# Two layers on one core: the order of seven weight products, and a tile of its own for a sum of weights

## The chip, the cores and the metric

The kernel runs on one core of one Trainium2 chip. TensorE (PE) multiplies matrices, VectorE (DVE) and ScalarE (ACT) do elementwise work, GpSimd (POOL) and SyncE (SP) mostly start transfers. The metric is the device time of one execution in microseconds (us). Beside the plain times there is one profiled execution, whose trace records what every engine did and when; all times within the program are counted from the start of its span.

## The reference

Two layers over 512 frames of width 1024, all in float32: the first with latent attention, the second with chunked attention, each followed by a SwiGLU feed-forward of inner width 2816. The feed-forward, which the change touches, is

```python
def rms_norm(x, g):
    xf = x.astype(jnp.float32)
    y = xf * lax.rsqrt(jnp.mean(xf * xf, axis=-1, keepdims=True) + EPS)
    return (y * g.astype(jnp.float32)).astype(x.dtype)
...
def swiglu(h, w_gate, w_up, w_down):
    return (jax.nn.silu(h @ w_gate) * (h @ w_up)) @ w_down
...
    for layer in range(DEPTH):
        h = rms_norm(x, attn_pre_g[layer])
        ...
        x = x + rms_norm(y, attn_post_g[layer])
        h = rms_norm(x, ffn_pre_g[layer])
        f = swiglu(h, ffn_w_gate[layer], ffn_w_up[layer], ffn_w_down[layer])
        x = x + rms_norm(f, ffn_post_g[layer])
```

## The kernel before

**Three matmuls for one.** A float32 operand is kept as a high part `hi` (rounded by a ScalarE cast, L144) and a low part `lo` (the rest, a VectorE subtraction, L145). Every product is hi·hi + lo·hi + hi·lo, three matmuls into the same bank of PSUM, the memory in which TensorE accumulates.

**Seven products for a pair of blocks.** The inner width 2816 is cut in 22 blocks of 128. The first four blocks are multiplied plainly (`proj`, L361 to L363; their gate is multiplied by the norm's factor at L1148, and L1151 forms the hidden block `hd`). The other 18 go in nine pairs of a gate and an up block through `products`. There the four quarter products of gate and up by the two halves of the frames (A0 and A1, 256 each) are had from seven products instead of eight, in Strassen's manner: sums of weights and sums of activations are multiplied, and the results are added up. Product j multiplies a weight tile `raw[j]` of 128x1024 by one of the lists in `moving`; it has two halves e of 12 matmuls each, which go to two banks. The banks are `be` for j0, `al` for j1, `ga` for j2, `al` for j3, j4 and j5, and `be` for j6. Several products thus accumulate in one pair of banks, and each is read out before the next is added to it: j0 and j1 by ScalarE copies (L1503, L1505), j2 by a VectorE addition to `gt` (L1507), j3 by a ScalarE copy to `gt` (L1509), j4 by a VectorE addition to `ut` (L1511), j5 by a ScalarE copy to `ut` (L1513), and j6 by a VectorE addition (L1515), which is followed by the norm's factor (L1516), silu (L1517), the product of gate and up (`hd`, L1519) and four sums of hidden blocks for the next stage (L1220 to L1223). `al` and `ga` come from a pool of four banks, which the plain blocks use as well, `be` from one of two other pairs of banks in turn.

**The weights.** Class `Pair` loads four tiles a pair (`tile`, L162, 512 KB each, started on SP's queue) and forms the others as sums on VectorE (L174): r0 = r4 + r5, r3 = r0 + r1, r6 = r3 + r2, and r4 becomes r4 + r1. r0, r3 and r6 share one tile ("sum", two buffers), since each is added in place to the one before. r4 lies in "sum2" (two buffers), r5, r1 and r2 in "raw" (five buffers). A load can start when a buffer is free, that is, when the last cast of its old contents is done.

**What sets the order.** `Feed` holds a plan: a list of all weight tiles in the order in which they are multiplied. `feed.next(1024, 2)` hands out the next one and, ahead of it, has the tile two places on split in hi and lo (with its sum) and the loads up to four places on started. The instructions of each engine are then put in an order by a scheduler with priorities, so that instructions of j6 may come ahead of those of j5, or those of one pair ahead of those of another. Each engine runs its list strictly in that order and waits where an operand is missing.

Behind `products` follows `down` (L1255), the last projection by a seven-product scheme of its own. In layer 1, `aside` runs beside `products`: it is advanced at the places where j is 1, 3 and 5, and brings the residual stream back in order of frames.

Of the kernel before, what the change touches and what calls it, by code (L numbers as in the profile page):

```python
# [10 lines left out]
F32 = mybir.dt.float32  # L11
# [7 lines left out]
D, S, P = 1024, 512, 128  # L19
# [49 lines left out]
def trunk(ctx: ExitStack, tc: tile.TileContext, a, out):  # L69
# [12 lines left out]
    def name_(n):  # L82
        uid[0] += 1
        return f"{n}_{uid[0]}"

    def U(dt=F32, name="u"):
        return up.tile([P, S], dt, tag="u", name=name_(name), bufs=NU)
# [4 lines left out]
    def bank(tag="mm", name="b"):  # L92
        return ps.tile([P, S], F32, tag=tag, name=name_(name), bufs={"mm": 4, "s": 2, "t": 2}[tag])
# [57 lines left out]
    class Pair:  # L151

        def __init__(self, src):
            self.src, self.raw = src, {}

# [13 lines left out]
        def sums(self, j):  # L172
            def plus(t, x, y):
                V.tensor_tensor(t, x, y, op=OP.add)  # L174

            r = self.raw
            if j == 0:
                r[0] = r[3] = r[6] = wide[0].tile([P, 1024], F32, tag="sum", name=name_("raw"), bufs=2)
                plus(r[0], r[4], r[5])
            elif j in (3, 6):  # L180
                plus(r[j], r[j], r[j // 3])
            elif j == 4:
                plus(r[4], r[4], r[1])

    wide = [None]

    class Down:
# [41 lines left out]
        def plus(self, j, i, x, y):  # L229

            x, t = self.at[x, i], self.at[y, i]
            n = max(len(x), len(t))
            cut_ = lambda v: v if len(v) == n else [v[0][:, c * S:c * S + S] for c in range(n)]
            for p, q in zip(cut_(t), cut_(x)):
                V.tensor_tensor(p, p, q, op=OP.add)
            self.at[j, i] = t
# [15 lines left out]
    class Feed:  # L252
# [8 lines left out]

        def add_pair(self, src):

            for j in range(7):
                self.plan.append((Pair(src) if not j else self.plan[-1][0], 1024, j, None))

        def add_down(self, src):
            d = Down(src)
# [73 lines left out]
        def next(self, n, ahead=True):  # L342
            i = self.pos
            self.pos += 1
            assert self.plan[i][1] == n
            self.split(i + int(ahead))
            return self.ready[i]
# [48 lines left out]
    def cut(t, c):  # L396
        return t[0][:, c], t[1][:, c]
# [97 lines left out]
    class Head:  # L495
# [3 lines left out]
        def __init__(self, qk, bt, scale, pv, sums):  # L499
            self.qk, self.bt, self.scale, self.pv, self.sums = qk, bt, scale, pv, sums  # L500
            self.p, self.pt = {}, None
# [538 lines left out]
    def start_a(h):  # L1040
# [12 lines left out]
        def pv(pth, ptl):  # L1053
            fill.until("v")
            o = bank()
            v_ = slice(h * VD, (h + 1) * VD)
            for kt in range(NQT):
                q_ = slice(kt * P, S)
                mm3(o[:, q_], (va[kt][:, 0, v_], va[kt][:, 1, v_]), (pth[:, kt, q_], ptl[:, kt, q_]),
                    kt == 0, kt == NQT - 1)  # L1060
            V.reciprocal(sums, sums)
            of = U(name="of")
            nc.scalar.copy(of, o)

            def rest():
                V.tensor_tensor(of, of, spread(sums), op=OP.mult)
                oh, ol = U(F32R, "oh"), U(F32R, "ol")
                split(oh, ol, of)
                osp.append((oh, ol))

            return rest
# [11 lines left out]
    def ffn(i, x_src, osp, firsts, late=()):  # L1083
# [55 lines left out]
        for f in range(N_WHOLE):  # L1139
# [13 lines left out]
            if f == 1:  # L1153
                next(more)
        products(xs, tb, rb, hid, by_tokens(H) if i else None)
        post = (AfterLast if i else After)(i, eps, H)
        down(hid, post)
# [311 lines left out]
    def products(xs, tb, rb, hid, aside=None):  # L1469

        K2 = KT // 2
        moving = [[cut(tb[k][0], A0) for k in range(K2)], [cut(xs[k], A0) for k in range(K2)],
                  [cut(xs[k + K2], A0) for k in range(K2)], [cut(tb[k][0], A1) for k in range(K2)],
                  [cut(tb[k][1], A0) for k in range(K2)], [cut(tb[k][1], A1) for k in range(K2)],
                  [cut(xs[k + K2], A1) for k in range(K2)]]
        pairs = (NF - N_WHOLE) // 2
        for p in range(pairs):
            al, ga = [], []
            be = [bank("t" if p % 2 else "s", "be") for _ in range(2)]
            gate = [U(name="gt") for _ in range(2)]  # L1480
            up_ = [U(name="ut") for _ in range(2)]
            for j in range(7):
                if aside is not None and j in (1, 3, 5):
                    next(aside, None)
                w = feed.next(1024, 2)
                if p + 1 == pairs and j >= 4:
                    hid.ahead(j // 5)
                if j == 1:
                    al = [bank(name="al") for _ in range(2)]
                if j == 2:  # L1490
                    ga = [bank(name="ga") for _ in range(2)]
                to = (be, al, ga, al, al, al, be)[j]
                for e in range(2):
                    o = to[e][:, A0]
                    for k in range(K2):
                        l, r = w(e * S + k * P, P), moving[j][k]
                        first_ = j < 3 and k == 0
                        for n, (c, d) in enumerate(((0, 0), (0, 1), (1, 0))):
                            nc.tensor.matmul(o, l[c], r[d], start=first_ and n == 0, stop=k == K2 - 1 and n == 2,  # L1499
                                             skip_group_check=True)  # L1500
                    t, u = gate[e], up_[e]
                    if j == 0:
                        nc.scalar.copy(u[:, A1], o)  # L1503
                    elif j == 1:
                        nc.scalar.copy(t[:, A0], o)  # L1505
                    elif j == 2:
                        V.tensor_tensor(t[:, A0], t[:, A0], o, op=OP.add)  # L1507
                    elif j == 3:
                        nc.scalar.copy(t[:, A1], o)  # L1509
                    elif j == 4:  # L1510
                        V.tensor_tensor(u[:, A1], o, u[:, A1], op=OP.add)  # L1511
                    elif j == 5:
                        nc.scalar.copy(u[:, A0], o)  # L1513
                    else:
                        V.tensor_tensor(t[:, A1], t[:, A1], o, op=OP.add)  # L1515
                        V.tensor_tensor(t, t, rb, op=OP.mult)  # L1516
                        nc.scalar.activation(t, t, AF.Silu)  # L1517
                        h = hid.room()
                        V.tensor_tensor(h, t, u, op=OP.mult)  # L1519
                        hid.add(h)  # L1520
# [274 lines left out]
```

## Time and profile before

| | us |
|---|---|
| median of 3 runs | 1112.13 (1111.6 to 1112.59) |
| the profiled execution | 1113.16 |
| its span | 1111.4 |
| `products` of layer 0 in it | 236.24 to 416.92 |
| `products` of layer 1 in it | 817.43 to 997.90 |

The span runs from the first instruction to the last; 1.8 us of the profiled execution lie around it. A row of a timeline gives the start in the span, the length, the engine, the line in the code, the operation, what is written and read, the sizes, how many instructions are joined in the row, and in brackets how long the engine was idle before it and whom it waited for. Matmuls overlap: each is shown until its last result is written, while the next one has long begun, so the distance from start to start is what one costs. The chain of waits follows the work that ended last back through the program, and its rows give start, length and the run of instructions that it passed through.

The busy times of L174 on VectorE and what it waited for, by the page's costliest groups:

```profile
L174 DVE TENSOR_TENSOR raw<-raw,raw 128x1024 f32<-128x1024 f32 x72 | 86.9, 1218 | 2.5 <-DMA raw<-in_w_pair 2.2
```

72 sums are 4 a pair in 18 pairs, 1218 ns each.

### The profile page before, as it was taken

The page shows a single profiled execution, that of the slowest core. Times are in us where ns is not written, and L with a number is a line of the kernel's source. Part 1 is how long each engine was busy: PE and PEld are TensorE (multiplying, and loading weights), DVE is VectorE, ACT ScalarE, POOL GpSimd, SP SyncE. Part 2 cuts the span into 40 slices and gives each one's busy share as a digit, 9 for nine tenths or more (in the row PEclk, how much of TensorE's full clock was granted, in tenths as well). Part 3 has the DMA queues.
Part 4 walks back from the last instruction along what each step waited for, and adds up shares of the span by engine and source line. Part 5 has one row for each costly group of instructions (what it writes and reads, how often), then busy time and mean ns, then how long its engine had stood idle before and what let it go on. Part 6 is the DMA issues. An engine that isn't in the chain of part 4 may idle for free.

```text
span 1111.4 us, 18953 instructions
## 1 busy us (share of the span) xinstructions
PE 1098.7 (99%) x6941; PEld 980.9 (88%) x6941; DVE 936.2 (84%) x1679; ACT 682.5 (61%) x1331; POOL 68.3 (6%) x106
## 2 busy tenths in 40 slices
PE   9999999999999999999999999999999999999997
PEld 6888889999999998888888888889999999998885
DVE  7788737999989989978868887758999999989977
ACT  6476636755555556668635777657755555556675
POOL 1200000000000001400000000000000000002402
PEclk9999999999999999999999999999999999999999
DMA  7432216323232357961556565635334444558913
GB/s 238 113 111 77 77 63 222 134 63 110 95 133 96 108 183 236 157 198 40 190 152 170 142 175 151 169 97 189 134 104 123 132 137 124 150 192 244 173 29 76
DMA packets 79885, 152.93 MB, mean 138 GB/s; under 512 B 25328, under 2 KB 27120, under 8 KB 79792
## 3 DMA queue, kind: packets, MB, share of 16 engines
q1 hardware_dynamic: 72448, 138.71, 40.2%
q0 software_dynamic: 6912, 12.59, 6.9%
q8 instruction: 54, 0.88, 0.3%
q10 hardware_dynamic: 432, 0.44, 0.1%
q14 instruction: 39, 0.32, 0.1%
HBM read 120.56 MB, written 10.68 MB: 118 GB/s over the span
## 4 chain that ended last, share of the span: by engine, by line
PE 90%; DVE 5%; DMA 2%; issue 2%; ACT 1%; POOL 0%; DVEq 0%; POOLq 0%; SPq 0%; ACTq 0%
PE al L1499 17%; PE b L361 11%; PE b L362 11%; PE b L363 11%; PE be L1499 8%; PE al L1255 8%; PE be L1255 5%; PE ga L1499 4%; PE de L1255 3%; PE ga L1255 3%; PE pt L523 2%; DVE wlo L145 2%; DMA x<-in_x 1%; DMA raw<-in_w_pair 1%; PE b L1655 1%
## 5 line engine op out<-in xcount | busy, mean ns | idle before, releaser
L144 ACT CAST whi<-raw 128x1024 fp32r<-128x1024 f32 (+3 forms) x224 | 225.2, 1007 | 199.0 <-PE al L1499 65.1
L145 DVE TENSOR_TENSOR wlo<-raw,whi 128x1024 fp32r<-128x1024 f32 (+3 forms) x224 | 260.2, 1164 | 44.8 <-ACT whi L144 43.7
L1499 PE MATMUL al<-th,whi 128*128 128x256 f32 x432 | 122.9, 285 | 0.5 <-DVE ut L1511 0.5
L1499 PE MATMUL al<-th,wlo 128*128 128x256 f32 x432 | 121.0, 281 | 0.3 <-DVE wlo L145 0.3
L1499 PE MATMUL al<-tl,whi 128*128 128x256 f32 x432 | 120.9, 280 | 0.0
L361 PE MATMUL b<-xh,whi 128*128 128x512 f32 (+1 forms) x298 | 114.6, 386 | 0.4 <-ACT whi L144 0.4
L363 PE MATMUL b<-xh,wlo 128*128 128x512 f32 (+1 forms) x298 | 110.3, 370 | 0.3 <-DVE wlo L145 0.3
L362 PE MATMUL b<-xl,whi 128*128 128x512 f32 (+1 forms) x298 | 109.9, 369 | 0.0
L174 DVE TENSOR_TENSOR raw<-raw,raw 128x1024 f32<-128x1024 f32 x72 | 86.9, 1218 | 2.5 <-DMA raw<-in_w_pair 2.2
L1499 PEld LDWEIGHTS al<-th,whi 128*128 128x128 f32 x432 | 81.3, 188 | 2.8 <-DVE ut L1511 0.9
L1499 PEld LDWEIGHTS al<-th,wlo 128*128 128x128 f32 x432 | 81.2, 188 | 0.6 <-DVE wlo L145 0.5
L1499 PEld LDWEIGHTS al<-tl,whi 128*128 128x128 f32 x432 | 81.3, 188 | 0.0
L511 ACT ACTIVATE p<-p,mn 128x128 f32<-128x128 f32 (+1 forms) x96 | 54.0, 562 | 39.3 <-DVE mn L509 38.4
L145 DVE TENSOR_TENSOR ptl<-pt,pth 128x128 fp32r<-128x128 f32 (+1 forms) x96 | 46.6, 486 | 29.4 <-ACT pth L144 23.7
L145 DVE TENSOR_TENSOR wlo<-wd,whi 128x512 fp32r<-128x512 f32 x86 | 56.3, 685 | 14.7 <-ACT whi L144 14.4
L363 PEld LDWEIGHTS b<-xh,wlo 128*128 128x128 f32 x298 | 56.2, 189 | 10.8 <-DVE wlo L145 1.2
L144 ACT CAST whi<-wd 128x512 fp32r<-128x512 f32 x86 | 49.8, 618 | 25.0 <-PE al L1255 10.7
L361 PEld LDWEIGHTS b<-xh,whi 128*128 128x128 f32 x298 | 56.5, 189 | 6.7 <-ACT whi L144 0.9
L362 PEld LDWEIGHTS b<-xl,whi 128*128 128x128 f32 x298 | 56.5, 190 | 5.8 <-DVE xl L149 0.2
L144 ACT CAST pth<-pt 128x128 fp32r<-128x128 f32 (+1 forms) x96 | 40.3, 421 | 26.8 <-PE pt L523 26.0
L1255 PE MATMUL al<-whi,pl 128*128 128x512 f32 x132 | 51.5, 390 | 0.0
L1255 PE MATMUL al<-whi,ph 128*128 128x512 f32 x132 | 51.4, 389 | 0.0
(313 smaller groups left out, 3266.8 us busy)
## 6 DMA issues: line engine op xcount, KB each, us to landing
raw<-in_w_pair SPq DMA_DIRECT2D x72, 512.0 KB, 3.8
wd<-in_w_down SPq DMA_DIRECT2D x54, 256.0 KB, 5.8
raw<-in_w_o SPq DMA_DIRECT2D x16, 512.0 KB, 3.6
raw<-in_w_gu SPq DMA_DIRECT2D x16, 512.0 KB, 4.2
raw<-in_w_down SPq DMA_DIRECT2D x16, 512.0 KB, 4.3
raw<-in_w_qkb SPq DMA_DIRECT2D x16, 512.0 KB, 3.5
wd<-in_w_down POOLq DMA_DIRECT2D x22, 256.0 KB, 5.2
wd<-raw POOLq DMA_DIRECT2D x22, 256.0 KB, 4.6
```

Source lines behind the costliest of these rows:

```text
L144: return (nc.scalar.copy(dst_hi, src), V.tensor_tensor(dst_lo, src, dst_hi.bitcast(F32), op=OP.subtract))
L145: V.tensor_tensor(dst_lo, src, dst_hi.bitcast(F32), op=OP.subtract))
L174: V.tensor_tensor(t, x, y, op=OP.add)
L361: nc.tensor.matmul(o, l[0], r[0], start=start, stop=False)
L362: nc.tensor.matmul(o, l[0], r[1], start=False, stop=False)
L363: last_mm[0] = nc.tensor.matmul(o, l[1], r[0], start=False, stop=stop)
L511: nc.scalar.activation(p[:, :n], p[:, :n], AF.Exp, bias=mn[:, :1], scale=-1.0, accum_out=self.sums[:, qt:qt + 1])
L523: nc.tensor.transpose(t[:, kt * P:(kt + 1) * P], p[:, kt * P:(kt + 1) * P], ident)
L1255: nc.tensor.matmul(to[e], l[c], r[d], start=j < 4 and k == 0 and n == 0, stop=k == NF // 2 - 1 and n == 2, skip_group_check=True)
L1499: nc.tensor.matmul(o, l[c], r[d], start=first_ and n == 0, stop=k == K2 - 1 and n == 2, skip_group_check=True)
L1655: nc.tensor.matmul(o[:, q_], vv, ptl[:, kt, q_], start=False, stop=kt == NQT - 1)
```

## The change

The seven products of a pair are planned and run in the order 1, 0, 3, 2, 4, 5, 6 in place of 0 to 6. The banks are then used in the order al, be, al, ga, al, al, be; of neighbouring products only j4 and j5 share banks, where before j3, j4 and j5 stood behind each other in `al`. r0 and r3 each get a "sum" tile (the pool has two buffers as before), r3 is written to its own tile, and r6 is formed in the tile of r2. Loading and `aside` go on hanging on j, not on the place.

```diff
+        ORDER = (1, 0, 3, 2, 4, 5, 6)
+
...
             r = self.raw
+            if j in (0, 3):
+                r[j] = wide[0].tile([P, 1024], F32, tag="sum", name=name_("raw"), bufs=2)
             if j == 0:
-                r[0] = r[3] = r[6] = wide[0].tile([P, 1024], F32, tag="sum", name=name_("raw"), bufs=2)
                 plus(r[0], r[4], r[5])
-            elif j in (3, 6):
-                plus(r[j], r[j], r[j // 3])
+            elif j == 3:
+                plus(r[3], r[0], r[1])
             elif j == 4:
                 plus(r[4], r[4], r[1])
+            elif j == 6:
+                r[6] = r[2]
+                plus(r[6], r[6], r[3])
...
-            for j in range(7):
-                self.plan.append((Pair(src) if not j else self.plan[-1][0], 1024, j, None))
+            pair = Pair(src)
+            for j in Pair.ORDER:
+                self.plan.append((pair, 1024, j, None))
...
-            for j in range(7):
+            for j in Pair.ORDER:
                 if aside is not None and j in (1, 3, 5):
                     next(aside, None)
```

Behind the changed lines the numbers are higher by 2 in `sums` (L174 is L176), by 7 in `products` and `Hidden.add` (L1499 is L1506, L1511 is L1518). The engines issue as many instructions as before. Three places show what moves.

VectorE in the fifth pair of layer 0, around the evictions of j4 (`ut`) into `ut_3846` and `ut_3847`; a `raw` on the left is a sum of weights, and `raw_4262` is the first sum r0 of a pair two further on. Before:

```order
L174 TENSOR_TENSOR raw_3768<-raw_3768,raw_3705 128x1024
L145 TENSOR_TENSOR wlo_3919<-raw_3633,whi_3918 128x1024
L1507 TENSOR_TENSOR gt_3844<-gt_3844,ga_3922 128x256
L1507 TENSOR_TENSOR gt_3845<-gt_3845,ga_3923 128x256
L145 TENSOR_TENSOR wlo_3953<-raw_3635,whi_3952 128x1024
L145 TENSOR_TENSOR wlo_3984<-raw_3768,whi_3983 128x1024
L1511 TENSOR_TENSOR ut_3846<-al_3887,ut_3846 128x256
L174 TENSOR_TENSOR raw_4262<-raw_4127,raw_4129 128x1024
L1511 TENSOR_TENSOR ut_3847<-al_3888,ut_3847 128x256
```

The same place now (the tiles have other numbers):

```order
L176 TENSOR_TENSOR raw_4102<-raw_4048,raw_3886 128x1024
L145 TENSOR_TENSOR wlo_3954<-raw_3674,whi_3953 128x1024
L1514 TENSOR_TENSOR gt_3848<-gt_3848,ga_3957 128x256
L1514 TENSOR_TENSOR gt_3849<-gt_3849,ga_3958 128x256
L145 TENSOR_TENSOR wlo_3989<-raw_3739,whi_3988 128x1024
L1518 TENSOR_TENSOR ut_3850<-al_3858,ut_3850 128x256
L176 TENSOR_TENSOR raw_3918<-raw_3918,raw_3886 128x1024
L1518 TENSOR_TENSOR ut_3851<-al_3859,ut_3851 128x256
```

Between the two evictions there stands a sum as before, but it is now r4 + r1 of the next pair, whose tiles are older. The first sum has gone to the end of a pair, among the last steps of `gt` and `hd`, here in the fourth pair:

```order
L1522 TENSOR_TENSOR gt_3602<-gt_3602,be_3600 128x256
L176 TENSOR_TENSOR raw_4048<-raw_3918,raw_3920 128x1024
L1523 TENSOR_TENSOR gt_3602<-gt_3602,bc_2704 128x512
L1522 TENSOR_TENSOR gt_3603<-gt_3603,be_3601 128x256
L145 TENSOR_TENSOR wlo_3855<-raw_3852,whi_3854 128x1024
```

ScalarE in the fifth pair, around the copies of j3 out of `al`. Before, with a cast between the two copies and j4 behind them in the same banks:

```order
L1505 COPY gt_3845<-al_3888 128x256
L144 CAST whi_3952<-raw_3635 128x1024
L1509 COPY gt_3844<-al_3887 128x256
L144 CAST whi_3983<-raw_3768 128x1024
L1509 COPY gt_3845<-al_3888 128x256
```

Now j3's copies are followed by j2's product in `ga`, and then by j4:

```order
L1516 COPY gt_3848<-al_3858 128x256
L144 CAST whi_3953<-raw_3674 128x1024
L1516 COPY gt_3849<-al_3859 128x256
L144 CAST whi_3988<-raw_3739 128x1024
L144 CAST whi_4018<-raw_3886 128x1024
L1520 COPY ut_3850<-al_3858 128x256
```

The cast still stands between the copies, but the next matmuls into `al` come a product later.

TensorE at the start of `products` in layer 0, behind the last plain block (`b`). Before, the 24 matmuls of j0 in `be` came first, then `al`. Now:

```order
L370 MATMUL b_2779<-xh_2267,wlo_2784 128x512
L368 MATMUL b_2780<-xh_2267,whi_2783 128x512
L369 MATMUL b_2780<-xl_2268,whi_2783 128x512
L370 MATMUL b_2780<-xh_2267,wlo_2784 128x512
L1506 MATMUL be_2848<-th_2594,whi_2856 128x256
L1506 MATMUL be_2848<-tl_2595,whi_2856 128x256
L1506 MATMUL be_2848<-th_2594,wlo_2857 128x256
L1506 MATMUL al_2866<-xh_2225,whi_2811 128x256
L1506 MATMUL al_2866<-xl_2226,whi_2811 128x256
```

Three matmuls of j0 stand ahead of the first of j1, the other 21 behind j1's 24. And between j4 and j5 of the sixth pair of layer 0, where before `al` followed `al` without a break, matmuls of j6 stand now:

```order
L1506 MATMUL al_4109<-th_2608,wlo_4174 128x256
L1506 MATMUL be_4096<-xh_2249,whi_4238 128x256
L1506 MATMUL be_4096<-xl_2250,whi_4238 128x256
L1506 MATMUL be_4097<-xh_2249,whi_4238 128x256
L1506 MATMUL be_4097<-xl_2250,whi_4238 128x256
L1506 MATMUL be_4096<-xh_2249,wlo_4239 128x256
L1506 MATMUL be_4096<-xh_2255,whi_4238 128x256
L1506 MATMUL be_4096<-xl_2256,whi_4238 128x256
L1506 MATMUL be_4096<-xh_2255,wlo_4239 128x256
L1506 MATMUL al_4108<-th_2596,whi_4203 128x256
```

By the order of all matmuls, one to eight such rows stand there in seven pairs of layer 0 and in five of layer 1; in the other six pairs j5 follows j4 directly.

## The prediction

> **What bounds the kernel now.** I read the page first, then the totals of the products in both layers, then the chain of waits, then single handoffs. From the page, the busy times and the granted TensorE clock in 40 slices:
>
> ```profile
> PE 1098.7 (99%) x6941; PEld 980.9 (88%) x6941; DVE 936.2 (84%) x1679; ACT 682.5 (61%) x1331; POOL 68.3 (6%) x106
> PEclk9999999999999999999999999999999999999999
> ```
>
> TensorE is the bound, at full clock everywhere. A matmul stays busy past the start of the next, so the 99% hides short waits; they must be read from the distance between starts. The only stages that the change touches are the two stretches of `products`. The windows view, for line 1499 alone (stretch; length, TensorE busy; weight loads; clock; DMA share; GB/s):
>
> ```profile
> 236.24:416.92 180.68, 180.17 (x1512) 178.61 (x1511) 1.00 0.36 118
> 817.43:997.90 180.47, 180.14 (x1512) 178.74 (x1511) 1.00 0.47 141
> ```
>
> What would these stretches last without any wait? The chain of waits gives the answer, each row being a start, a length and a run of matmuls on one kind of bank. A run of 72 is j3, j4, j5 of one pair:
>
> ```profile
> 305.80 8.64 PE al L1499 x72
> ...
> 405.54 8.69 PE al L1499 x72
> ...
> 866.44 8.45 PE al L1499 x72
> ...
> 891.99 0.60 PE be L1499 x4
> 892.59 2.91 PE al L1499 x24
> ```
>
> The run at 866.44 has no wait: 8.45/72 = 0.1174 us a matmul. 3024 matmuls at 0.1174 are 355.0 us; the two stretches take 361.15. So **at most about 6.1 us, 0.55% of the program, can be won here**, and only if every wait goes. Gaps over 0.14 us between starts hold 5.05 us of it (worked out below by kind); the rest is a pitch a little longer than 0.1174, which the change doesn't touch.
>
> **The largest kind: j3 to j4 in one bank.** j4 accumulates into the two `al` banks that j3 has just filled, after ScalarE has copied j3 out. One handoff, fifth pair of layer 0, second bank; timelines of TensorE and of ScalarE:
>
> ```profile
> 329.65 0.28 PE L1499 MATMUL al<-th,wlo 128*128 128x256 f32 x1
> 329.86 0.38 PE L1499 MATMUL al<-th,whi 128*128 128x256 f32 x1
> 330.08 0.28 PE L1499 MATMUL al<-tl,whi 128*128 128x256 f32 x1
> ...
> 328.49 1.05 ACT L144 CAST whi<-raw 128x1024 fp32r<-128x1024 f32 x1 [0.96 <-PE al L1499]
> 329.45 0.36 ACT L1509 COPY gt<-al 128x256 f32<-128x256 f32 x1
> ```
>
> Starts lie 0.21 and 0.22 apart instead of 0.12: the copy ends at 329.81, 0.09 us after the matmul could have started, and one more step is late by 0.10, a refill. The copy was late because a cast of 1.05 us stood ahead of it. So 0.19 us each. Rows of the chain with 8.64 to 8.69 in place of 8.45 are these; eight pairs of layer 0 and five of layer 1 have it: 13 × 0.19 = **2.5 us**. [...]
>
> **The second kind: a sum held by a DMA.** In the second and third pair of layer 0 the first sum of a later pair stands on VectorE between the two evictions of j4 and waits for its weights:
>
> ```profile
> 270.67 1.23 DVE L174 TENSOR_TENSOR raw<-raw,raw 128x1024 f32<-128x1024 f32 x1 [0.55 <-DMA raw<-in_w_pair]
> 271.81 0.42 DVE L1511 TENSOR_TENSOR ut<-al,ut 128x256 f32<-128x256 f32 x1
> ...
> 271.68 0.28 PE L1499 MATMUL al<-th,wlo 128*128 128x256 f32 x1
> 272.29 0.39 PE L1499 MATMUL al<-th,whi 128*128 128x256 f32 x1 [0.33 <-DVE ut L1511]
> 272.52 0.28 PE L1499 MATMUL al<-tl,whi 128*128 128x256 f32 x1
> ...
> 292.40 0.28 PE L1499 MATMUL al<-th,wlo 128*128 128x256 f32 x1
> 292.86 0.38 PE L1499 MATMUL al<-th,whi 128*128 128x256 f32 x1 [0.18 <-DVE ut L1511]
> 293.08 0.28 PE L1499 MATMUL al<-tl,whi 128*128 128x256 f32 x1
> ```
>
> 272.29 − 271.68 − 0.12 = 0.49, with the refill 0.60; the second 0.34 + 0.10 = 0.45: **1.05 us**.
>
> **The third kind** is the start of layer 1 and the pairs of layer 1 in which `be` matmuls are already mixed in.
>
> ```profile
> 826.07 0.28 PE L1499 MATMUL al<-tl,whi 128*128 128x256 f32 x1
> 826.68 0.39 PE L1499 MATMUL al<-th,wlo 128*128 128x256 f32 x1 [0.33 <-DVE wlo L145]
> ```
>
> 0.61 − 0.12 and a refill of 0.11: 0.60. In the chain above, the run at 891.99 takes 0.60 for 4 (0.47 without a wait) and the next 2.91 for 24 (2.82): 0.2, three times, 0.6. Smaller ones of 0.07 to 0.10: 0.3. Together **1.5 us**, and 2.5 + 1.05 + 1.5 = 5.05.
>
> **The change part by part.** The counts don't change: every engine issues as many instructions of the same shapes before and after, so no busy time is added. What changes is order and one tile.
>
> (a) *Order of products.* Banks now run al, be, al, ga, al, al, be. Between j3 and j4 lie the 24 `ga` matmuls, 24 × 0.1174 = 2.8 us, against a copy late by 0.09: the 13 waits go, −2.5. Between j1 and j3 lie 24 `be` matmuls, as much cover for the copy of j1. In their place j4 to j5 is next in line. It is not a new handoff but was covered by the very stall removed. VectorE and TensorE in the same pair before:
>
> ```profile
> 330.72 0.42 DVE L1511 TENSOR_TENSOR ut<-al,ut 128x256 f32<-128x256 f32 x1
> 331.05 1.22 DVE L174 TENSOR_TENSOR raw<-raw,raw 128x1024 f32<-128x1024 f32 x1
> 332.18 0.42 DVE L1511 TENSOR_TENSOR ut<-al,ut 128x256 f32<-128x256 f32 x1
> ...
> 331.39 0.28 PE L1499 MATMUL al<-th,whi 128*128 128x256 f32 x1
> 332.81 0.28 PE L1499 MATMUL al<-th,whi 128*128 128x256 f32 x1
> ```
>
> The evictions end at 331.14 and 332.60; j5 starts at 331.39 and 332.81, and 0.19 earlier without the stall, at 331.20 and 332.62. With the 0.05 that lie between a copy's end and the matmul (329.81 to 329.86), it is ready at 331.19 and 332.65: on the edge, and an edge costs at least the refill. The order of the changed kernel puts `be` matmuls of j6 between j4 and j5 in 12 of 18 pairs (one to eight), each a cover of 0.12; those I cost at nothing, except two with five of them in which a sum and a `wlo` are queued ahead of the evictions of j4 on VectorE, at the 0.2 of 891.99. Six pairs have no `be` ahead of j5. A wait there costs between nothing and the 0.60 of a sum caught at the same place; I take 0.17, next to the 0.19 of row 329.86, since what is ahead of the eviction is a sum that isn't late. 6 × 0.17 + 2 × 0.2 = **+1.4**.
>
> (b) *The first sum moves.* It goes from between the evictions of j4 to the end of a pair, some 5.7 us later. Its DMAs move too, on SP's queue behind the same casts.
>
> ```profile
> DMA to landing us min/median/max: 3.1/3.8/6.1
> ```
>
> An estimate: its last tile is issued behind the `wlo` cast of the fifth product, 5 × 2.8 = 14 us into a pair of 20, and by this row lands 17 to 20 us into it; the sum is wanted at 19.5. No wait, or one of half a microsecond on VectorE that no matmul awaits, since the `lo` part of the next product is cast two products ahead (5.6 us). So −1.05. If that cover goes, 0.45 to 0.60 returns in each pair it hits. The sum's own tile only changes where the result goes: 1.2 us before and after.
>
> (c) *Start of each layer.* Here lies the price. `al` comes after three or four `be` matmuls, where 24 stood before, and needs two banks that the gate and up blocks still hold. VectorE, and windows by engine: the stage ahead, the first pair and a steady pair (TensorE, weight loads, VectorE, ScalarE, GpSimd):
>
> ```profile
> 236.64 1.28 DVE L1148 TENSOR_TENSOR gt<-b,bc 128x512 f32<-128x512 f32 x2
> 237.83 1.22 DVE L145 TENSOR_TENSOR wlo<-raw,whi 128x1024 fp32r<-128x1024 f32 x1
> 238.97 1.28 DVE L1151 SCALAR_TENSOR_TENSOR hd<-gt,b 128x512 f32<-128x512 f32 x2
> ...
> 215.00:236.00 21.00, 21.00 (x97) 17.22 (x97) 19.48 (x41) 13.72 (x23) 1.45 (x1) 1.00 0.19 63
> 236.00:256.30 20.30, 20.30 (x172) 20.19 (x171) 19.55 (x27) 11.31 (x18) 0.00 (x0) 1.00 0.33 104
> 334.40:354.47 20.07, 20.07 (x170) 19.95 (x170) 18.40 (x26) 10.99 (x18) 0.00 (x0) 1.00 0.32 105
> ```
>
> The first `al` would start at 236.24 + 3 × 0.12 = 236.6. The first of the two `gt<-b` at 236.64 frees a bank at about 237.3 at the latest; if it frees the one that `al` takes, the wait is up to 0.7, less what the order shifts. VectorE has 1.5 us free of 21 in the stage ahead, into which the first sum (1.2) now comes, so it may run later than now. Ends: nothing if the multiplication comes first, 3.5 if `al` takes a bank that only `hd` frees (worked out with the rivals). I take 0.45 in layer 0, between 0 and 0.7 and nearer to the upper row, and 0.2 in layer 1, where the order gives one more `be`: **+0.65**.
>
> **Sum.** −5.05 + 1.4 + 0.65 = −3.0 us. The profiled execution took 1113.16 us (span 1111.4 and 1.8 around it); 1113.16 − 3.0 = 1110.2. It lies 1.03 above the median of 1112.13, so a median of **1109.1 us**.
>
> **Rivals.**
>
> *The wait moves to j4 and j5 in every pair.* For it: the edge above, and that `be` in between can itself wait for its `wlo` (891.99). Against: 866.44, where j4 to j5 ran without any. 18 × 0.15 (near the 0.19) = 2.7, and the starts 0.65: −5.05 + 3.35 = −1.7, so 1110.4. Chance 0.24.
>
> *Slower: the start of each layer stands still.* Mechanism: `al` gets a bank that only `hd` at 238.97 frees (first of two, about 239.6), and the first sum of 1.2 us is queued ahead of it. From 236.6 that is 3.0 + 1.2 = 4.2, less 0.7 for `hd` coming one place earlier, 3.5 a layer, 7 for both, with j4 to j5 as forecast +1.4: −5.05 + 8.4 = +3.4, about 1115.5. It decides once the bank is freed after about 239 (a wait over 2.5). Against it: the multiplication frees banks two microseconds earlier, and the scheduler's order puts it ahead. Chance 0.11.
>
> *All waits go:* −5.05 and no new one, 1107.1. For it: 866.44. Against: the edge and the three `be`. Chance 0.08.
>
> [...] Chance 0.01.
>
> **How the numbers follow.** Forecast 0.56, rivals 0.24, 0.11, 0.08 and 0.01. A difference of 0.2%, 2.2 us, is about the least that a measurement of this kernel tells from no change. The forecast's own range, from the bounds of (a) and (c), is −4.4 to −0.9: mostly beyond 2.2. Faster by over 0.2%: 0.60 (0.45 of the forecast, 0.08 of all waits gone, 0.07 of the moved waits). Within: 0.27 (0.11, and 0.16 of the moved waits). Slower: 0.13 (0.11, the clock 0.01, and 0.01 of the moved waits). Range: up to 1113.0, which takes in the moved waits at 0.19 and a start that stands still for two thirds of its 7 us, and down to 1106.6, all waits gone and half a microsecond of the longer pitch.
>
> **What would show it.** In the changed kernel's timeline the first matmul of j4 starts 0.12 after the last of `ga`, and no sum of weights waits for a DMA in the first three pairs: then (a) and (b) hold. Runs of j4 and j5 of 5.63 in the chain, with be in between, bear out the 12 covered pairs; 0.2 more in all of them is the first rival. The distance between the third `be` and the first `al` of a layer is (c): 0.5 was priced, 2.5 or more is the slower rival. The prediction is wrong if the two stretches of products do not shorten from 361.15 to about 358.

## The result, and the profile after

The changed kernel takes **1122.94 us** (median of 4 runs, 1121.58 to 1124.0) against 1112.36 us of the kernel before (4 runs): a ratio of 1.0097, 95% interval 1.0085 to 1.0109. It is slower by some 10.6 us where 3 us less were forecast, and lies outside the range. The profiled execution took 1124.0 us, its span 1121.5. The page of after, busy times and granted clock:

```profile
PE 1103.0 (98%) x6941; PEld 985.2 (88%) x6941; DVE 935.6 (83%) x1679; ACT 681.5 (61%) x1331; POOL 74.8 (7%) x106
PEclk9999999999999999999999999999999999999999
```

Nobody does more work, but one number stands out: GpSimd (POOL) is busy for 74.8 us with 106 instructions, 68.3 before with as many. The windows view of after, for the products' line alone:

```profile
240.96:422.41 181.45, 181.23 (x1512) 180.43 (x1511) 1.00 0.35 115
827.17:1007.99 180.82, 180.33 (x1512) 178.92 (x1511) 1.00 0.45 136
```

The two stretches take 362.3 us, where 361.15 were shown before. So they did not shorten, and the lost 10 us lie elsewhere. Cutting both spans at the starts of the same instructions shows where, `bc` being the four small matmuls that spread the norm's factor r ahead of the plain blocks' gates:

| from start to start | before | after | more |
|---|---|---|---|
| span's start to `bc` of layer 0 | 220.76 | 223.88 | 3.12 |
| to the first product | 15.48 | 17.08 | 1.60 |
| to the last product | 180.56 | 181.17 | 0.61 |
| to `bc` of layer 1 | 384.99 | 387.95 | 2.96 |
| to the first product | 15.48 | 17.09 | 1.61 |
| to the last product | 180.37 | 180.54 | 0.17 |
| to the span's end | 113.75 | 113.74 | 0 |

9.3 of 10.1 us arise between a layer's norm and its first product, a stage that the prediction had set aside. TensorE's timeline there, after:

```profile
220.41 0.39 PE L370 MATMUL b<-xh,wlo 128*128 128x512 f32 x1
223.88 0.84 PE L491 MATMUL bc<-ident,r 128*128 128x128 f32 x4 [3.08 <-POOL r L474]
...
225.37 0.63 PE L370 MATMUL b<-xh,wlo 128*128 128x512 f32 x1
225.80 0.63 PE L368 MATMUL b<-xh,whi 128*128 128x512 f32 x1
```

TensorE stands still for 3.1 us until GpSimd has r, and then starts a matmul every 0.43 us in place of 0.23. The clock of that stretch, after (first row) and before, in windows of all engines:

```profile
224.30:228.50 4.20, 4.20 (x15) 3.34 (x14) 3.12 (x5) 3.02 (x4) 0.00 (x0) 0.61 0.16 63
```

```profile
224.30:228.50 4.20, 4.20 (x20) 3.49 (x19) 4.10 (x7) 2.39 (x4) 0.00 (x0) 1.00 0.34 125
```

The granted clock is 0.61 behind the wait. In the 40 slices of the profile's page, 28 us each, it doesn't show. And r itself, GpSimd's power of -1/2 over 128x4 numbers, after and before:

```profile
218.42 5.40 POOL L474 TENSOR_TENSOR r<-v,mhalf 128x4 f32<-128x4 f32 x1 [22.90 <-DVE eps L1138]
```

```profile
219.25 1.45 POOL L467 TENSOR_TENSOR r<-v,mhalf 128x4 f32<-128x4 f32 x1 [23.63 <-DVE eps L1131]
```

The same instruction starts 0.8 us earlier and takes 5.40 us in place of 1.45. Nothing in its own row says why. VectorE's rows at that time differ, after:

```profile
218.11 0.16 DVE L470 TENSOR_SCALAR v<-ss 128x4 f32<-128x4 f32 x1
...
218.59 0.42 DVE L145 TENSOR_TENSOR tl<-t,th 128x256 fp32r<-128x256 f32 x1
218.93 1.22 DVE L176 TENSOR_TENSOR raw<-raw,raw 128x1024 f32<-128x1024 f32 x1
220.06 0.42 DVE L145 TENSOR_TENSOR tl<-t,th 128x256 fp32r<-128x256 f32 x1
220.40 0.75 DVE L1289 SCALAR_TENSOR_TENSOR t<-t,xg 128x256 f32<-128x256 f32 x2
...
222.20 0.75 DVE L145 TENSOR_TENSOR tl<-t,th 128x256 fp32r<-128x256 f32 x2
225.38 1.29 DVE L1155 TENSOR_TENSOR gt<-b,bc 128x512 f32<-128x512 f32 x2 [2.42 <-ACT bc L498]
```

and before, with the ScalarE instruction that the second row waits for below it:

```profile
219.42 0.42 DVE L145 TENSOR_TENSOR tl<-t,th 128x256 fp32r<-128x256 f32 x1
219.79 0.43 DVE L1282 SCALAR_TENSOR_TENSOR t<-t,xg 128x256 f32<-128x256 f32 x1
220.13 0.42 DVE L145 TENSOR_TENSOR tl<-t,th 128x256 fp32r<-128x256 f32 x1
220.89 1.22 DVE L174 TENSOR_TENSOR raw<-raw,raw 128x1024 f32<-128x1024 f32 x1 [0.34 <-DMA raw<-in_w_pair]
...
219.04 0.72 ACT L1281 ACTIVATE xg<-x,gains 128x512 f32<-128x512 f32 x1
```

After, VectorE runs from `v` to 222.95 without a pause, and the power ends at 223.82, 0.87 us behind it. In layer 1 it is the same: 5.06 us after, 1.45 before.

Before, the power ended at 220.70. VectorE had paused at 220.55 for 0.34 us, because a sum of weights waited for its DMA, and it is tempting to see in this the way in. But 0.87 us back from 220.70 is 219.83, where the row at 219.42 ends, 0.7 us before that pause. There stands a much smaller one, which the timeline does not name: instructions of this size start 0.33 to 0.34 us apart, but the `t` at 219.79 starts 0.37 behind the row at 219.42. It needs `xg`, which ScalarE finished at 219.76. After, a sum stands at this place, r3 of the first pair, whose weights are long there, and when the next `t` comes at 220.40, its `xg` has long been there too. That the power got in at the small pause is read from the 0.87 us; no row shows the moment itself.

### The profile page after: what moved, and what is told of

It is laid out like the page before. It is cut to its first block, busy times and chain, and to the rows that moved or that the text cites. A ratio compares the mean times of both kernels' runs of the same rounds, so it can differ in the third digit from the quotient of the medians.

```text
span 1121.5 us, 18929 instructions
## 1 busy us (share of the span) xinstructions
PE 1103.0 (98%) x6941; PEld 985.2 (88%) x6941; DVE 935.6 (83%) x1679; ACT 681.5 (61%) x1331; POOL 74.8 (7%) x106
## 5 line engine op out<-in xcount | busy, mean ns | idle before, releaser
L1506 PE MATMUL al<-th,whi 128*128 128x256 f32 x432 | 122.1, 283 | 0.0
L1506 PE MATMUL al<-tl,whi 128*128 128x256 f32 x432 | 121.4, 281 | 0.0
L1506 PE MATMUL al<-th,wlo 128*128 128x256 f32 x432 | 121.4, 281 | 0.0
L176 DVE TENSOR_TENSOR raw<-raw,raw 128x1024 f32<-128x1024 f32 x72 | 87.3, 1215 | 0.0
L1506 PEld LDWEIGHTS al<-th,whi 128*128 128x128 f32 x432 | 81.7, 189 | 0.5 <-DVE ut L1518 0.2
L1506 PEld LDWEIGHTS al<-th,wlo 128*128 128x128 f32 x432 | 81.7, 189 | 0.0
L1506 PEld LDWEIGHTS al<-tl,whi 128*128 128x128 f32 x432 | 81.7, 189 | 0.0
```

## The experiments

**Theory A**: VectorE's unbroken run shuts GpSimd out, and the power gets through in the next pause. **Theory B**: the power is slow for a reason of its own. A third view puts the loss on the order of the products. In the notes below, a power's two times are those of layers 0 and 1.

**A pause by force.** VectorE waits for r right behind `v`:

```diff
         V.tensor_scalar(eps, ss, EPS / D, EPS * EPS, op0=OP.mult, op1=OP.add)
+        with first(300):
+            V.tensor_copy(small("pz")[:, :4], r)
         some(rest, 7)
```

> The changed kernel, with one more VectorE instruction of 128x4 that reads the factor r as soon as GpSimd's power has made it, so that VectorE stands idle from about 0.3 us behind v until r is there. Theory A (VectorE's unbroken run of instructions with two operands in SBUF shuts GpSimd out, and the power only comes to an end when VectorE pauses): the power takes 1.0 to 1.5 us in place of 5.4 and 5.1, TensorE's wait of 3.1 to 3.2 us ahead of bc goes in both layers and with it the ten matmuls at half rate behind it (1.6 to 1.8 us a layer): some 10 us less than the change, 1112 to 1114 us. Theory B (the power is slow or late for a reason of its own, and VectorE doesn't matter): the power stays at 5 us, and VectorE's wait for it comes on top, 1123 to 1127 us.

1114.26 us (1113.37 to 1114.73, 10 runs), ratio to the kernel before 1.0015 (1.0005 to 1.0024). GpSimd's row:

```profile
218.40 1.12 POOL L474 TENSOR_TENSOR r<-v,mhalf 128x4 f32<-128x4 f32 x1 [22.89 <-DVE eps L1138]
```

1.12 us in both layers, TensorE no longer waits for `bc`, and 8.7 of the 10.6 us are back; the time lies just above the 1112 to 1114 us that A forecast. B falls. The pause itself costs VectorE about 0.9 us a layer, and the way from `bc` to the first product is 0.5 to 0.6 us longer than before.

**The pause of the kernel before, taken away.** There the first sum of the second pair is issued later:

```diff
-                plus(r[0], r[4], r[5])
+                seen[0] += 1
+                with tc.issue_after(plain[0].ins) if seen[0] % 9 == 2 else ExitStack():
+                    plus(r[0], r[4], r[5])
```

(`plain[0]` is the last low part of the plain blocks' weights.)

> The kernel before, with one sum of weights a layer moved: the first sum of the second pair, for whose DMA VectorE stood idle for 0.34 us (layer 0) and 0.14 us (layer 1) behind v, is issued six places later, behind the two products of gate and norm. No work is added, and a wait of VectorE is taken away. Theory A: without that pause the power lasts until VectorE's run ends, some 3.5 to 4.5 us, TensorE waits 2 to 3 us for bc in each layer and then runs ten matmuls at half rate: 1119 to 1122 us, nearly the whole loss of the change without any of it. Theory B, or the loss coming from the order of the products: 1111 to 1113 us.

1112.26 us (1110.93 to 1116.51, 10 runs), ratio 0.9999 (0.9990 to 1.0009): the forecast of theory A missed. The power is still 1.45 us long, from 218.81 to 220.26. VectorE's rows:

```profile
218.98 0.42 DVE L145 TENSOR_TENSOR tl<-t,th 128x256 fp32r<-128x256 f32 x1
219.35 0.42 DVE L1287 SCALAR_TENSOR_TENSOR t<-t,xg 128x256 f32<-128x256 f32 x1
...
220.27 0.43 DVE L1287 SCALAR_TENSOR_TENSOR t<-t,xg 128x256 f32<-128x256 f32 x1 [0.16 <-ACT xg L1286]
```

The wait for the DMA is gone, but the small wait for `xg` is not: `t` starts 0.37 us behind `tl` again, and 0.87 us before the power's end is 219.39, the end of that `tl`. (The wait of 0.16 us at 220.11 comes too late, as the one for the DMA did before.) So the run took away a pause that did not matter, and as a test of the unbroken run it failed.

**The order alone, and the tile alone.** In the first the sums stay in place in one tile; in the second `ORDER` is (0, 1, 2, 3, 4, 5, 6).

```diff
-            if j in (0, 3):
-                r[j] = wide[0].tile([P, 1024], F32, tag="sum", name=name_("raw"), bufs=2)
             if j == 0:
+                r[0] = r[3] = r[6] = wide[0].tile([P, 1024], F32, tag="sum", name=name_("raw"), bufs=2)
                 plus(r[0], r[4], r[5])
-            elif j == 3:
-                plus(r[3], r[0], r[1])
+            elif j in (3, 6):
+                plus(r[j], r[j], r[j // 3])
```

> The order 1, 0, 3, 2, 4, 5, 6 alone, with the sums formed in place in one tile as before. The sum behind v is then r4 + r1 of the first pair, whose weights are long there. Theory A: no pause, so the same loss as with the whole change, 1121 to 1124 us, and a power of about 5 us. If the loss came from the tile of its own: 1110 to 1112 us.

> A tile of its own for the first sum alone, in the old order 0 to 6. The sum behind v is r4 + r1 of the first pair here too, without a wait for a DMA. Theory A: the power of about 5 us and the loss of 4.5 to 5 us a layer, 1121 to 1123 us, though no matmul of the pairs is moved. If the loss came from the order of the products: 1111 to 1113 us.

The order alone: 1122.8 us (1122.47 to 1123.56), ratio 1.0095 (1.0078 to 1.0112), powers of 5.40 and 5.07 us. The tile alone: 1119.57 us (1118.52 to 1120.94), ratio 1.0065 (1.0050 to 1.0080), powers of 4.73 us in both layers, though its products run in the old order. That is 7 us more than before, a little less than the 1121 to 1123 us that A forecast. Either part puts a sum whose weights are there ahead of the `t` that waited for ScalarE, and either pays. The two losses are one and the same, paid once. Layer 0 of the order alone also shows that the slow clock is not bound to follow: the same wait, and full rate behind it.

```profile
223.68 0.65 PE L487 MATMUL bc<-ident,r 128*128 128x128 f32 x4 [3.08 <-POOL r L470]
...
224.20:228.40 4.20, 4.20 (x21) 3.45 (x20) 3.42 (x5) 3.11 (x5) 0.00 (x0) 1.00 0.14 57
```

**The repair.** In the changed kernel r3 and r4 + r1 wait for the last low part of the plain blocks' weights, so that VectorE's row behind `v` is the one that waits for ScalarE's `xg` in the run with the moved sum.

```diff
-                plus(r[3], r[0], r[1])
+                with tc.issue_after(plain[0].ins):
+                    plus(r[3], r[0], r[1])
             elif j == 4:
-                plus(r[4], r[4], r[1])
+                with tc.issue_after(plain[0].ins):
+                    plus(r[4], r[4], r[1])
```

> The whole change, with the sums r3 and r4 + r1 issued only behind the last low part of the plain blocks' weights: in the first pair of each layer they move from right behind v to behind the two products of gate and norm, and VectorE's row behind v is what it was in the run with the moved sum of the kernel before. Theory A: VectorE waits for ScalarE there once, as in that run, the power ends after 1.45 us, and TensorE's wait for bc and the half rate behind it go in both layers: 1110 to 1113 us, 10 us below the change. If those two sums delay the freeing of banks (they stand ahead of hd), 1 to 2 us of it come back at the start of the pairs. Theory B (the power slow for itself, or the order of the products to blame): 1121 to 1124 us.

> The old order 0 to 6 with a tile of its own for the first sum, and the same two sums issued behind the last low part of the plain blocks' weights. Theory A: the 7 us that the tile alone cost go, 1110 to 1113 us; the waits from j3 to j4 (13 or more of 0.19 us) stay, those of a sum held by a DMA go. Theory B: 1118 to 1121 us as with the tile alone.

The change so repaired: 1113.08 us (1112.17 to 1114.1, 11 runs), ratio 1.0008 (0.9999 to 1.0017). The tile alone so repaired: 1112.31 us (1111.43 to 1113.59, 11 runs), ratio 1.0003 (0.9994 to 1.0012). The first lies just above the 1110 to 1113 us of the forecast, the second inside it. The power takes 1.45 us in all four places, and no `bc` waits for it:

```profile
218.75 1.45 POOL L479 TENSOR_TENSOR r<-v,mhalf 128x4 f32<-128x4 f32 x1 [22.90 <-DVE eps L1143]
...
220.96 0.60 PE L496 MATMUL bc<-ident,r 128*128 128x128 f32 x4
```

With the two sums held back the loss is gone, whatever the order. But the order brings nothing either, which the forecast of 3 us has to answer for.

**The power beside runs of one kind.** Two kernels that compute nothing of the layers time the same power beside runs of VectorE, all of it twice over.

```python
    STREAMS = (("alone", None, 0, 0), ("twoin", both, 12, 256), ("large", both, 4, 1024), ("onein", one_in, 12, 256),
               ("short", both, 4, 256))
...
    STREAMS = (("alone", None, ()), ("small", both, (S,) * 12), ("medium", both, (M,) * 7), ("large", both, (L,) * 4),
               ("first", both, (L,) + (S,) * 9), ("later", both, (S, S, L) + (S,) * 8),
               ("bank", from_bank, (M,) * 7), ("single", single, (L,) * 4),
               ("row", both, (S, S, L, S, S, S, L, S, S)))
```

`both` adds two tiles in SBUF, `one_in` and `from_bank` a bank of PSUM and a tile, `single` scales one tile; S, M and L are 256, 512 and 1024 columns.

> Nothing of the layers is computed; one power of 128x4 on GpSimd is timed five times, twice over, each time beside another run of VectorE additions that starts right behind v: none; twelve of 128x256 with both operands in SBUF (some 4 us); four of 128x1024 with both in SBUF (4.6 us); twelve of 128x256 with one operand in PSUM; four of 128x256 with both in SBUF (1.4 us). Theory A: alone about 1.0 us; beside the twelve and the four large ones until their end, 4 to 5 us; beside those with one operand in PSUM about 1.0 us; beside the short run about 2 us. If only large additions shut GpSimd out: 1.0 us beside the twelve of 128x256, over 4 beside the large ones. Theory B: 1.0 us in all five.

> Nothing of the layers is computed; the power of 128x4 (1.01 us alone) is timed beside nine runs of VectorE instructions that start right behind v, twice over. In the first such kernel twelve additions of 128x256 left it at 1.0 to 1.1 us and four of 128x1024 held it until 0.87 us behind their end (5.3 us). Theory A1 (a single large instruction with two operands in SBUF is enough: GpSimd then waits for the end of the whole unbroken run behind it, small ones too): one large followed by nine small 5.0 us; two small, one large, eight small 5.3 us; the changed kernel's row (two small, large, three small, large, two small) 5.4 us. Theory A2 (GpSimd is held for the length of a large instruction alone): 2.0, 2.0 to 2.8 and 2.0 to 4 us. Seven of 128x512: over 4.5 us if 0.6 us is large enough, else 1.1. Seven of 128x512 with one operand in PSUM and four of 128x1024 with one operand at all: 1.0 us, if the second SBUF operand is what matters; if length matters, 4.5 us.

GpSimd's timeline in the first, and VectorE's beside two of its powers:

```profile
1.22 1.01 POOL L47 TENSOR_TENSOR ralone<-v_alone,mhalf 128x4 f32<-128x4 f32 x1 [0.39 <-DVE v_alone L45]
...
9.48 5.32 POOL L47 TENSOR_TENSOR rlarge<-v_large,mhalf 128x4 f32<-128x4 f32 x1 [3.64 <-DVE v_large L45]
15.08 1.01 POOL L47 TENSOR_TENSOR ronein<-v_onein,mhalf 128x4 f32<-128x4 f32 x1 [0.28 <-DVE v_onein L45]
...
21.82 1.11 POOL L47 TENSOR_TENSOR rtwoin<-v_twoin,mhalf 128x4 f32<-128x4 f32 x1 [0.28 <-DVE v_twoin L45]
...
9.31 4.62 DVE L35 TENSOR_TENSOR t<-a,b 128x1024 f32<-128x1024 f32 x4
14.91 4.06 DVE L38 TENSOR_TENSOR t<-bank,b 128x256 f32<-128x256 f32 x12
```

Beside the four large additions the power ends at 14.80, 0.87 us behind their end at 13.93, the same 0.87 as in the changed kernel. Beside twelve small ones with an operand in PSUM it takes 1.01 us, as if alone. But beside twelve small ones with both operands in SBUF it takes 1.11, and beside four of them 1.11 too where 2 were forecast, against theory A. The second kernel, with the run of scalings on VectorE in the last row:

```profile
9.40 4.99 POOL L53 TENSOR_TENSOR rmedium<-v_medium,mhalf 128x4 f32<-128x4 f32 x1 [3.64 <-DVE v_medium L51]
14.68 1.91 POOL L53 TENSOR_TENSOR rlarge<-v_large,mhalf 128x4 f32<-128x4 f32 x1 [0.28 <-DVE v_large L51]
19.29 1.92 POOL L53 TENSOR_TENSOR rfirst<-v_first,mhalf 128x4 f32<-128x4 f32 x1 [2.70 <-DVE v_first L51]
23.51 5.27 POOL L53 TENSOR_TENSOR rlater<-v_later,mhalf 128x4 f32<-128x4 f32 x1 [2.31 <-DVE v_later L51]
29.06 1.01 POOL L53 TENSOR_TENSOR rbank<-v_bank,mhalf 128x4 f32<-128x4 f32 x1 [0.28 <-DVE v_bank L51]
33.32 1.76 POOL L53 TENSOR_TENSOR rsingle<-v_single,mhalf 128x4 f32<-128x4 f32 x1 [3.24 <-DVE v_single L51]
35.79 1.11 POOL L53 TENSOR_TENSOR rrow<-v_row,mhalf 128x4 f32<-128x4 f32 x1 [0.72 <-DVE v_row L51]
...
33.15 2.49 DVE L41 TENSOR_SCALAR t<-a 128x1024 f32<-128x1024 f32 x4
```

The power beside the same four large additions now takes 1.91 us, beside one large and nine small 1.92, beside two small and a large one with eight small behind 5.27, and beside the changed kernel's row copied in sizes 1.11. Each of these came again in the second round, within 0.01. So neither size nor length decides, and neither A1 nor A2 holds. Wherever both operands are in SBUF and VectorE runs on, the power ends 0.86 to 0.87 us behind the end of one of VectorE's instructions: the first one (1.11, 1.91 and 1.92) or the last of the row. What decides between the two these runs don't show. With one operand in PSUM it took 1.01 us all four times. Beside `single`, with one operand at all, 1.0 had been forecast and 1.76 came, both times: beside scalings of one tile in SBUF it is longer too, but it ends at 35.08, ahead of the end of the row (35.64).

**The sums in pieces of 128x256,** a test in the kernel of whether one large instruction is what it takes:

```diff
             def plus(t, x, y):
-                V.tensor_tensor(t, x, y, op=OP.add)
+                for c in range(0, 1024, 256 if j in (3, 4) else 1024):
+                    c_ = slice(c, c + (256 if j in (3, 4) else 1024))
+                    V.tensor_tensor(t[:, c_], x[:, c_], y[:, c_], op=OP.add)
```

> The whole change, with r3 and r4 + r1 formed in four pieces of 128x256 in place of one addition of 128x1024 (the same work in 108 more VectorE instructions). Behind v there then stand ten instructions of 128x256 before the first of 128x1024. Theory A1 or A2: the power is done before the large one, in 1.0 to 1.5 us, TensorE does not wait for bc, 1111 to 1114 us. If any unbroken run of VectorE holds GpSimd: 4 to 5 us for the power and 1120 to 1124 us.

1122.2 us (1119.6 to 1124.37), ratio 1.0091 (1.0074 to 1.0108), with powers of 5.61 and 5.28 us:

```profile
217.72 5.61 POOL L476 TENSOR_TENSOR r<-v,mhalf 128x4 f32<-128x4 f32 x1 [22.89 <-DVE eps L1140]
```

In layer 0 eleven small instructions stand between `eps` and the first large one, and they hold GpSimd as the large one does; the theories that a large instruction is needed fall in the kernel too. The run without a pause stays: in the four kernels without the small wait for `xg` (the change, the order alone, the tile alone, the pieces) the power was held to the end of VectorE's row in all eight places, and in the five with it (the kernel before, the moved sum, the two repairs and the last experiment below) it took 1.45 us in all ten.

**No neighbours in one bank.** With `bc` repaired, are the waits between products worth anything? The repair, with j6 ahead of j5:

```diff
-        ORDER = (1, 0, 3, 2, 4, 5, 6)
+        ORDER = (1, 0, 3, 2, 4, 6, 5)
...
-                    elif j == 5:
-                        nc.scalar.copy(u[:, A0], o)
-                    else:
+                    elif j == 6:
                         V.tensor_tensor(t[:, A1], t[:, A1], o, op=OP.add)
                         V.tensor_tensor(t, t, rb, op=OP.mult)
                         nc.scalar.activation(t, t, AF.Silu)
+                    else:
+                        nc.scalar.copy(u[:, A0], o)
                         h = hid.room()
```

> The whole change with the two sums held back as in the repair, and in the order 1, 0, 3, 2, 4, 6, 5: no neighbouring products share banks any more, and the hidden block is finished behind j5 in place of j6. What is tested is whether waits between products are still worth anything once bc doesn't wait. If the sum of the waits sets the length of the two stretches: the gaps between starts in them fall from the 3.4 us of the repair to about 1 to 2 us, and the time to 1110.5 to 1112 us, below both kernels. If the pitch of the matmuls between the waits (117.3, 118.7 or 120.0 ns, which changes only at a wait) decides as much as the waits: fewer waits and no gain, 1112 to 1114 us.

**1106.53 us** (1105.53 to 1109.08, 5 runs), ratio to the kernel before 0.9959 (0.9945 to 0.9973): faster than both kernels, and by more than either view forecast. Windows of it, the products' line alone:

```profile
235.05:412.62 177.57, 177.57 (x1512) 177.36 (x1511) 1.00 0.36 118
812.40:990.05 177.65, 177.65 (x1512) 177.42 (x1511) 1.00 0.46 143
```

355.2 us for both stretches, where the prediction had put a floor of 355.0. In the whole trace of them one wait is left, 0.08 us long, and the `wlo` waits described below are gone with the others. What the new order shares with the repair is the way in for GpSimd; what it adds, 6.5 us against the repair, lies in these stretches (361.6 us in the repair, 355.2 here).

## Why the prediction was wrong, point by point

**The step that failed** is the sentence "The only stages that the change touches are the two stretches of `products`", and with it the reading of part (c): "VectorE has 1.5 us free of 21 in the stage ahead, into which the first sum (1.2) now comes, so it may run later than now." The sums of a layer's first pairs are formed in the stage ahead, and the change puts one that is ready, r3 of the first pair, ahead of a `t` at which VectorE used to wait for ScalarE, right behind `v`. I looked for what the sum would be late for on VectorE, and not for who works beside VectorE at that place. That price is 3.0 us of waiting a layer, and 1.6 more where the clock falls: 9.3 us. It was no term of the sum and no rival. The slower rival did stand at the start of each layer, but by another mechanism, banks freed late by `hd`, which did not occur.

**(b) The first sum moves** came out as said. VectorE no longer waits for a DMA ahead of a sum; the costliest groups of after show 0.0 us of idle time where 2.5 stood:

```profile
L176 DVE TENSOR_TENSOR raw<-raw,raw 128x1024 f32<-128x1024 f32 x72 | 87.3, 1215 | 0.0
```

Two of these waits had cost TensorE 1.05 us, as priced. The harm came with the other sums: with the new order, or with the new tile, one of the first pair's sums is ready early and fills the place at which GpSimd had got in.

**(a) The order** took the waits from j3 to j4 away, as priced: the trace of after has none. The gaps between starts in both stretches fell from 5.05 to 3.5 us, by 1.5; the forecast was a fall by 3.0, to the 1.4 and 0.65 of new ones. j4 to j5 in the same banks cost 0.04 to 0.3 at a place, 1.05 in all. What was mis-sized are the `be` matmuls between j4 and j5, "each a cover of 0.12; those I cost at nothing". They belong to j6, whose low part is not yet there:

```profile
356.12 0.28 PE L1506 MATMUL be<-xl,whi 128*128 128x256 f32 x1
356.61 0.39 PE L1506 MATMUL be<-xh,wlo 128*128 128x256 f32 x1 [0.21 <-DVE wlo L145]
...
355.34 1.22 DVE L145 TENSOR_TENSOR wlo<-raw,whi 128x1024 fp32r<-128x1024 f32 x1
```

0.49 from start to start, 0.37 too much, and 0.1 more at the step behind it: waits of this kind make up 2.5 of the 3.5 us. They come in the seven pairs with five or more `be` matmuls between j4 and j5, and in none with fewer. The rows of layer 1 before (891.99) had shown the kind; I took 0.2 for two pairs of it where seven pay 0.2 to 0.5.

**(c) The start of a layer** costs nothing: `al` follows the third `be` at 0.12. 0.65 had been priced.

**The rest of the sum.** "The rest is a pitch a little longer than 0.1174, which the change doesn't touch" was wrong too. A count of matmuls in a stretch without waits, first after, then in the last experiment:

```profile
256.00:336.00 80.00, 80.00 (x669) 80.00 (x668) 1.00 0.33 106
```

```profile
256.00:336.00 80.00, 80.00 (x684) 80.00 (x684) 1.00 0.33 106
```

15 matmuls fewer in 80 us, 120.0 ns from start to start in place of 117.3. The mean pitch of the two stretches, gaps left out, was 117.7 and 117.8 before, 119.2 and 117.9 after, 118.3 and 118.4 in the repair; 3024 × 0.6 ns are 1.8 us, as much as the repair had saved in gaps (5.05 to 3.4). So the order with its remaining waits gains nothing, and the order almost without waits gains 5.9 us in the two stretches, nearly all that the floor allowed.

**The clock behind the wait.** In the four kernels with the wait for r, TensorE was idle for 2.7 to 3.3 us at each of eight places. Behind four of them the clock over the next 4.2 us was 0.50 to 0.64, with a matmul every 0.43 us; behind the other four it was 1.00, and the length of the wait does not tell them apart (half rate behind 2.75 us, full rate behind 3.29; behind 3.08 us 0.61 in layer 0 of the change and 1.00 in layer 0 of the order alone). What decides it is not shown. In the two stretches of products themselves the granted clock was 1.00 before, after and in the last experiment: none of these runs shows the fall of the clock to which the prediction gave 0.01. The same kernels scatter by up to 5 us from run to run, and in two of them the granted clock of the whole run goes with it: in the pieces 0.998 at 1119.6 us, 0.997 at 1121.25, 0.995 at 1123.15 and 0.994 at 1124.37, in the tile alone 0.998 at 1118.52 and 0.995 at 1120.94. In the changed kernel it does not (0.995 at 1121.58, 0.996 at 1124.0).

**What stays open.** That VectorE's row behind `v` decides is shown by the forced pause, by either part alone and by the repair. That it is the wait of 0.04 us for `xg` that lets GpSimd in is read from the traces alone; no run takes away or adds just this wait. Nor is it known why GpSimd gets in without any pause beside some runs of the small kernels and not beside others. For the pitch the ten traces of the whole program show this much: 18 of their 20 stretches have gaps of 1.15 to 3.8 us together, and their mean pitch is 117.6 to 119.2 ns and their length 179.5 to 181.5 us, however long the gaps; the two of the last experiment, with one wait of 0.08 us, stay at 117.3. Why is not shown.

## What to carry to other kernels

Going by these traces, an engine's short wait can be another engine's way in, even one too short to be named in a timeline (0.04 us here, with a power of 1.45 us beside it and up to 5.61 without it): before an instruction of VectorE is moved, look what GpSimd does at that time and who waits for it. When a pause is to explain something, check that it comes early enough. Going by these runs, small instructions on GpSimd that lie on the path of TensorE belong beside a pause of VectorE (1.12 us for the power), or beside additions that read one operand from PSUM (1.01 us). And price a change of order with the matmuls that will fill the gap: they need their own operands, which cost 0.2 to 0.5 us in seven pairs here. Here waits made fewer and shorter brought nothing, and the same waits removed brought nearly all.

## What the runs showed that I had not expected

- **GpSimd beside VectorE.** The power took 1.01 us alone in the small kernels and 1.01 beside additions with one operand in PSUM. Beside the scalings of one tile in SBUF it took 1.76 us; they start 0.60 us apart where additions of that size start 1.14 apart. Beside an unbroken row of additions of two tiles in SBUF it took up to 5.32 us, until VectorE paused, and sometimes only 1.11; in the whole program up to 5.61.
- **The pitch of matmuls changes at waits.** In the two stretches 128x256 matmuls ran between two waits at one of three constant pitches, 117.3, 118.7 or 120.0 ns, at a granted clock of 1.00, for up to 669 matmuls; a new pitch came only where one matmul started more than 0.124 us behind another. A stretch of 1512 without any wait stayed at 117.3.
